# Two of four pairs of gather buffers lent to the reading of weights until four blocks are multiplied

## The chip, the core and the metric

The kernel runs on one core of one Trainium2 chip. The metric is the device time of one launch in microseconds (us); less is better. The core has TensorE (PE in the rows; PEld is its weight load), VectorE (DVE), ScalarE (ACT), GpSimd (POOL) and SyncE (SP). SP issues the large reads of weights, GpSimd issues the gathers, and all of them are carried by the same 16 DMA engines.

## What is computed

Two transformer layers on 256 tokens of width 1024, in float32. Each layer has an attention and short-convolution part (the "mixer") and then a mixture of very many tiny experts, which is where the change lies:

```python
def peer(h, w_query, sub_keys, expert_u, expert_v):
    ...
    q = (hf @ w_query).reshape(T, PEER_HEADS, 2, PEER_HALF)
    scores = jnp.einsum("thpd,hpnd->thpn", q, sub_keys).astype(jnp.float32)
    top_v, top_i = lax.top_k(scores, PEER_TOPK)
    ...
    best_v, best_pos = lax.top_k(cand_v, PEER_TOPK)
    expert_idx = jnp.take_along_axis(cand_i, best_pos, axis=-1)
    gates = jax.nn.softmax(best_v, axis=-1).astype(h.dtype)
    ...
        u = jnp.take(expert_u, xc["idx"], axis=0)
        vv = jnp.take(expert_v, xc["idx"], axis=0)
        a = jax.nn.gelu(jnp.einsum("td,thkd->thk", xc["h"], u))
        return jnp.einsum("thk,thkd->td", xc["g"] * a, vv)
```

There are 16384 experts. Each is a row of 1024 numbers in `expert_u` (the first matrix) and one in `expert_v` (the second). Each token picks 128 of them: 8 heads with 16 each.

## The kernel before, in words

The two halves of the 256 tokens are handled in two ways. Tokens 0 to 127 are multiplied densely: all of the first matrix streams through TensorE (128 blocks of 128 experts), Gelu is taken of every product, the products are weighed by the gates, and then all of the second matrix streams through TensorE. Tokens 128 to 255 gather: for each of the 128 picks, GpSimd issues an indirect DMA that fetches one row of 4 KB for each of the 128 tokens (0.5 MB), and VectorE multiplies it; first 128 gathers of U rows in four quarters, then those of V rows, interleaved as in `GROUPS` (line 29).

**The stream of weights.** `stream` (lines 108 to 146) is the list of all weight loads in the order of their use. Its unit is a group of 1 MB (two blocks): for the expert part 8 groups of `w_query`, then 64 groups U0 to U63, then 64 groups V0 to V63. `load_ahead` (line 175) issues on SP's queue as many groups as there are buffers, and it is called again each time a group has been used up (`dense_done`, line 354). A group goes into a spare part if one fits, and otherwise into a ring of three `raw` buffers.

**Spare parts.** At the start of the expert part, memory that is needed only later is handed to the stream by `give_back` with a limit (lines 1205 to 1212). `spare_part` (line 157) lets a group take the first part, in the order of limits, whose limit is at least the group's place. The places are -8 to -1 for the 8 groups of `w_query` and 0 to 63 for U0 to U63 (line 151); V groups have none.

```python
def spare_part(i):
    if i in place:
        for j, (last, _) in enumerate(spare):
            if place[i] <= last:
                spare_of[i] = spare.pop(j)
                return spare_of[i][1]
```

The parts are eight 1 MB pieces of the two halves of the products (tiles `al` and `ah` in the rows), with limits 1, 9, 17, 25, 33, 41, 49 and 57; the four pairs of gather buffers (tile `rows`) with limit -5; and `hot` with limit 29. Parts of the same limit stand in the order in which they were handed over, the pieces of the halves first. A part that is given back can be taken again by a group whose place is within its limit.

**Gathers.** `experts` (line 954) holds the gather buffers in the list `free` (line 981), 8 of them, two in each pair. `issue` (line 983) takes as many buffers as are free and issues a gather into each, if the quarter's routing is done. `use` (line 1000) multiplies the oldest gather on VectorE (line 1005 for U, 1013 for V), frees its buffer and calls `issue`. From query block 9 on there is one `use` per block, and one per block of U.

**The order around the change.** `query` (line 911) multiplies 16 query blocks. After each, `step` (line 1047) lets VectorE do some routing (`route`, line 826: the top 16 lists, the gates, the indices), issues gathers and, from block 9 on, uses one. Then come the blocks of U (loop at line 1091): 8 matmuls each (line 1097), a share of routing while it lasts, one use; after four blocks ScalarE takes the Gelu (line 1111). When the routing is done, `factors` (line 895) turns the gates of the first half on TensorE (line 899) into `iT`, `jT` and `gT` (lines 901 and 903). From there on the products are weighed between the blocks (`weigh`, line 1073). The V loop (line 1132) follows; its loads are kept in step with the gathers by a small copy that VectorE releases (line 195).

Each engine runs its instructions in the order in which the program issues them.

Of the kernel before, what the change touches and what calls it, by code (L numbers as in the profile page):

```python
# [27 lines left out]
NROWS, MORE = 8, (1, 3)  # L28
# [18 lines left out]
def body(ctx: ExitStack, tc: tile.TileContext, d: dict, out: bass.AP):  # L47
# [11 lines left out]
    def open_h():  # L59
        split["h"] = split["stack"].enter_context(tc.tile_pool(name="hid", bufs=1))  # L60
# [6 lines left out]
    def mm_ps(shape):  # L67
        return psum.tile(shape, F32, name="mm", bufs=2)
# [86 lines left out]
    spare_of = {}  # L155
# [10 lines left out]
    def give_back(part):  # L166
        spare.append(part)
        spare.sort(key=lambda p: p[0])
# [6 lines left out]
    def load_ahead():  # L175

        while state["dma"] < len(stream):
            kind, parts = stream[state["dma"]]
            if state["dma"] < len(START):
                if state["out0"] == NRAW0:  # L180
                    return
                t = first.tile([128, 2, D], F32, name="raw0", bufs=NRAW0)
                state["out0"] += 1
            elif (t := spare_part(state["dma"])) is not None:
                pass
            elif state["out"] < NRAW:
                t = strm.tile([128, 2, D], F32, name="raw", bufs=NRAW)
                state["out"] += 1
            else:
                return  # L190
            if kind == "V" and in_step["on"]:

                mark = in_step["marks"][0:1, in_step["n"]:in_step["n"] + 1]
                in_step["n"] += 1
                V.memset(mark, 0.0)
                nc.sync.dma_start(mark, d["c"][:, 0:1])
            for s, ap in parts:
                nc.sync.dma_start(t[:, s], ap)
            raws[state["dma"]] = t
            state["dma"] += 1  # L200
# [52 lines left out]
    def tick():  # L253
        due = [x for x in later if x[0] <= 0]
        for x in due:
            later.remove(x)
            x[1]()
        for x in later:
            x[0] -= 1
# [6 lines left out]
    def gate_begin(l, r):  # L266
        acc = work.tile([128, D], F32, name=f"acc{r}")
        G.memset(acc, 0.0)
        nc.gpsimd.dma_start(acc[0:1], d["b_gate"][l, r:r + 1])
        acc_of[l, r] = acc  # L270
# [75 lines left out]
    def dense(kind):  # L346

        while isinstance(stream[state["unit"] // 2][0], tuple):
            next_unit()
        g = state["unit"] // 2  # L350
        assert stream[g][0] == kind and state["unit"] % 2 == 0
        return raws[g]

    def dense_done():
        g = state["unit"] // 2
        raws.pop(g)
        state["unit"] += 2
        if g in spare_of:
            give_back(spare_of.pop(g))
        else:  # L360
            state["out"] -= 1
        load_ahead()
# [5 lines left out]
    def fill(budget):  # L368
        credit[0] = min(credit[0] + budget, 4000.0)
        while bg and credit[0] > 0:  # L370
            cost = next(bg[0], -1)
            if cost is None:
                return
            if cost < 0:
                bg.popleft()
            else:
                credit[0] -= cost
# [253 lines left out]
    def norm_full(l, xps, hf):  # L631

        rr = rms_row()
        keep_warm(WARM[2])
        raw = dense("query")
        pss = [y_ps([128, S]) for _ in range(2)]
        for k in range(KD):
            z = work.tile([128, S], F32, name="hf", bufs=4)
            V.scalar_tensor_tensor(z, xps[k // 2][:, k % 2], acol[:, l, 1, k:k + 1], rr, op0=OP.mult, op1=OP.mult)
            A.activation(hf[:, k], z, AF.Identity, bias=adac[:, l, 2, k:k + 1])  # L640
            for x in range(2):
                T.matmul(pss[x], raw[:, x, k * 128:(k + 1) * 128], hf[:, k], start=(k == 0), stop=(k == KD - 1))
        dense_done()
        return pss
# [309 lines left out]
    def experts(es, xp, rp, low, halves, pairs, hot, l, hf, pss):  # L954
# [23 lines left out]
        ys = []  # L978
        seen = {"dve": False}

        free = deque(pair[:, i] for i in range(2) for pair in pairs)

        def issue():
            while tasks and free and tasks[0][1] in routed:
                assert not any(last < 0 for last, _ in spare_of.values())
                kind, q, s = tasks.popleft()
                t = free.popleft()
                s += 32 * q
                G.indirect_dma_start(out=t, out_offset=None, in_=rows[kind],  # L989
                                     in_offset=bass.IndirectOffsetOnAxis(ap=idx[:, s:s + 1], axis=0))  # L990
                flying.append((kind, q, s, t))
# [8 lines left out]
        def use():  # L1000
            if not flying:
                return
            kind, q, s, t = flying.popleft()
            if kind == "U":
                V.scalar_tensor_tensor(t, t, 1.0, h1, op0=OP.mult, op1=OP.mult, accum_out=av[:, s:s + 1])  # L1005
                if s % 32 == 31:
                    c = slice(32 * q, 32 * q + 32)
                    after(6, lambda: A.activation(cv[:, c], av[:, c], AF.Gelu_apprx_tanh))
                    after(9, lambda: weights(q))
            else:  # L1010
                assert q in ready_c
                if seen["dve"]:
                    V.scalar_tensor_tensor(y1, t, cv[:, s:s + 1], y1, op0=OP.mult, op1=OP.add)  # L1013
                else:
                    V.tensor_scalar(y1, t, cv[:, s:s + 1], None, op0=OP.mult)
                    seen["dve"] = True
            free.append(t)
            issue()
# [72 lines left out]
        for e in range(0, NE, 4):  # L1091
            ps = mm_ps([128, 4, 128])
            for u in range(0, 4, 2):
                raw = dense("U")
                for x in range(2):
                    for k in range(KD):
                        T.matmul(ps[:, u + x], raw[:, x, k * 128:(k + 1) * 128], hf[:, k, :128],  # L1097
                                 start=(k == 0), stop=(k == KD - 1))
                    if bg:
                        fill(1350)  # L1100
                    elif e >= 64:
                        i = e + u + x
                        while done[0] < 34 and done[0] * (NE - begun[0]) < 35 * (i + 1 - begun[0]):
                            next(weighing, None)
                            done[0] += 1
                    if bg or e < 64:
                        begun[0] = e + u + x + 1
                    use()
                    tick()
                dense_done()  # L1110
            A.activation(halves[e // 64][:, e % 64:e % 64 + 4], ps, AF.Gelu_apprx_tanh)  # L1111
        spare.clear()
        for _ in weighing:
# [18 lines left out]
        for e in range(0, NE, 2):  # L1132
# [19 lines left out]
            for x in range(2):  # L1152
                i = e + x
# [33 lines left out]
    for l in range(DEPTH):  # L1187
        if l:
            open_h()
        h = norm(l, 0, "qk", xps) if l else first_norm(xps)  # L1190
        gate_begin(l, 0)
        gate_begin(l, 1)
        early.close()
        pol["pool"] = POOL_MIX[l]
        with ExitStack() as es:
            xps = mixer(es.enter_context(tc.tile_pool(name="mix", bufs=1)), l, *h)
        es = ExitStack()
        xp = es.enter_context(tc.tile_pool(name="exp", bufs=1, side="right"))
        hf = xp.tile([128, KD, S], F32, name="hfull")
        split["stack"].close()  # L1200
        rp = es.enter_context(tc.tile_pool(name="route", bufs=1, side="right"))
        low = ExitStack()
        halves = [stack.enter_context(tc.tile_pool(name=f"act{n}", bufs=1, side="right", reuse_waits="tile"))
                  .tile([128, 64, 128], F32, name=f"a{n}") for n, stack in (("h", es), ("l", low))][::-1]
        for b in range(8):
            part = halves[b // 4][:, b % 4 * 16:b % 4 * 16 + 16].rearrange("p j t -> p (j t)")
            give_back((8 * b + 1, part.rearrange("p (u c) -> p u c", u=2)))
        pairs = [xp.tile([128, 2, D], F32, name=f"rows{i}") for i in range(NROWS // 2)]
        for t in pairs:
            give_back((-5, t))  # L1210
        hot = xp.tile([128, 9, 256], F32, name="hot")
        give_back((29, hot[:, :8].rearrange("p a b -> p (a b)").rearrange("p (u c) -> p u c", u=2)))
        load_ahead()
        pss = norm_full(l, xps, hf)
        xps = experts(es, xp, rp, low, halves, pairs, hot, l, hf, pss)
# [67 lines left out]
```

## Time and profile before

| | us |
|---|---|
| median of 3 runs | 1865.59 |
| lowest and highest | 1862.36, 1866.03 |
| the profiled execution's own time | 1870.19 |
| its span, first to last instruction | 1868.4 |

The mean granted clock of TensorE over the span is 0.948 of full speed. Busy shares of the span: TensorE 87%, VectorE 76%, GpSimd 51%, ScalarE 31%; the DMA engines move 669 MB, at a mean of 358 GB/s.

How to read it: an average over the whole span mixes stages that are limited by different engines. Busy times are therefore read by stretch, and a wait is read together with what ended it. Times within the execution count from the first instruction. The expert part of layer 0 lies from about 255 to 938 us; that of layer 1 starts some 907 us later.

### The profile page before, as it was taken

What the parts mean: (1) busy time and instruction counts of PE and PEld (TensorE: products, weight loads), DVE (VectorE), ACT (ScalarE), POOL (GpSimd) and SP (SyncE); (2) the same over time, 40 slices, a digit from 0 to 9 for tenths busy, and PEclk for the clock granted to TensorE, in tenths of its full rate; (3) what the DMA queues carried; (4) which work ended last, traced back from release to release, by engine and by line L of the source; (5) the groups of instructions that cost most, each with busy time, mean ns of one, the idle gap of its engine ahead of it and who ended that gap; (6) DMA issues with size and microseconds to landing.
All of it is one profiled execution on the core that took longest, in us unless ns stands there. A gap on an engine that the chain in (4) does not pass through costs nothing.

```text
span 1868.4 us, 26270 instructions
## 1 busy us (share of the span) xinstructions
PE 1620.5 (87%) x9527; PEld 1270.3 (68%) x9527; DVE 1414.8 (76%) x2723; ACT 575.8 (31%) x1257; POOL 951.1 (51%) x731
## 2 busy tenths in 40 slices
PE   6899889976879989987789999998786998988776
PEld 4779769976879744533357997898786994444322
DVE  7887859999978776655566967699997887666455
ACT  3464332211156433300046444221112654331001
POOL 3535203444579776755341231244446987776551
PEclk7899999988989999999999999999897999999999
DMA  8658788999999999999945676899999999999997
GB/s 318 252 193 320 260 336 307 404 408 409 408 391 392 409 415 416 415 415 414 410 169 198 251 288 256 327 384 408 409 404 382 389 402 415 411 416 414 415 416 283
DMA packets 163203, 669.24 MB, mean 358 GB/s; under 512 B 16001, under 2 KB 16001, under 8 KB 146690
## 3 DMA queue, kind: packets, MB, share of 16 engines
q1 hardware_dynamic: 87346, 396.39, 54.3%
q0 software_dynamic: 73856, 268.48, 36.3%
q10 hardware_dynamic: 1872, 2.69, 0.4%
q8 instruction: 75, 1.23, 0.3%
q14 instruction: 54, 0.44, 0.1%
HBM read 666.46 MB, written 1.05 MB: 357 GB/s over the span
## 4 chain that ended last, share of the span: by engine, by line
DVE 33%; DMA 29%; PE 23%; issue 6%; POOL 4%; ACT 3%; SPq 0%; POOLq 0%; ACTq 0%; DVEq 0%
DMA rows<-in_expert_v_dram,idx 16%; PE mm L1097 8%; DVE rows L1005 7%; DMA raw<-in_expert_v_dram 6%; PE yp L1155 4%; DVE raw L288 4%; DMA rows<-in_expert_rows_dram,idx 4%; PE wp L1084 3%; DVE y L1013 3%; POOL rows L989 3%; DVE wl L343 2%; PE mm L392 1%; PE mm L393 1%; PE mm L394 1%; PE mm L938 1%
## 5 line engine op out<-in xcount | busy, mean ns | idle before, releaser
L989 POOL DMA_INDIRECT rows<-in_expert_rows_dram,idx x256 | 306.8, 1198 | 335.3 <-DVE rows L1005 92.2
L989 POOL DMA_INDIRECT rows<-in_expert_v_dram,idx x256 | 329.4, 1287 | 231.5 <-DMA rows<-in_expert_v_dram,idx 95.7
L1013 DVE SCALAR_TENSOR_TENSOR y<-rows,cv,y 128x1024 f32<-128x1024 f32 x254 | 335.6, 1321 | 147.2 <-DMA rows<-in_expert_v_dram,idx 140.0
L1005 DVE SCALAR_TENSOR_TENSOR rows<-rows,h 128x1024 f32<-128x1024 f32 x256 | 329.2, 1303 | 3.5 <-DMA rows<-in_expert_rows_dram,idx 3.3
L1155 PE MATMUL yp<-raw,ah 128*128 128x512 f32 x512 | 242.3, 621 | 56.0 <-DMA raw<-in_expert_v_dram 54.8
L343 POOL TENSOR_TENSOR wl<-raw,wh 128x1024 fp32r<-128x1024 f32 x52 | 137.1, 2641 | 272.5 <-ACT wh L338 255.7
L1155 PE MATMUL yp<-raw,al 128*128 128x512 f32 x512 | 244.4, 622 | 32.1 <-DMA raw<-in_expert_v_dram 31.8
L1097 PE MATMUL mm<-hfull,raw 128*128 128x128 f32 x1984 | 241.1, 281 | 19.1 <-ACT al L1111 15.4
L1097 PEld LDWEIGHTS mm<-hfull,raw 128*128 128x128 f32 x1984 | 232.5, 196 | 19.9 <-ACT al L1111 15.8
L1069 ACT ACTIVATE hot<-iotf,iT 128x128 f32<-128x128 f32 x512 | 163.2, 390 | 262.6 <-PE wp L1084 229.0
L1155 PEld LDWEIGHTS yp<-raw,ah 128*128 128x128 f32 x512 | 96.1, 196 | 200.6 <-issue 101.3
L1097 PE MATMUL mm<-hfull,ah 128*128 128x128 f32 x1600 | 193.6, 283 | 14.9 <-ACT al L1111 14.9
L1097 PEld LDWEIGHTS mm<-hfull,ah 128*128 128x128 f32 x1600 | 190.1, 200 | 15.3 <-ACT al L1111 15.3
L1155 PEld LDWEIGHTS yp<-raw,al 128*128 128x128 f32 x512 | 95.0, 195 | 137.2 <-issue 96.9
L392 PE MATMUL mm<-hh,wh 128*128 128x256 f32 x512 | 150.4, 294 | 10.1 <-ACT qT L656 6.3
L1067 POOL TENSOR_TENSOR hot<-hot,gT 128x256 f32<-128x256 f32 x128 | 152.2, 1190 | 2.4
L1084 PEld LDWEIGHTS wp<-hot 128*128 128x128 f32 x1024 | 129.9, 193 | 32.4 <-issue 28.7
L338 ACT ACTIVATE wh<-raw 128x1024 fp32r<-128x1024 f32 x112 | 115.9, 1051 | 101.7 <-DMA raw<-in_w_gt_dram 39.4
L393 PE MATMUL mm<-hl,wh 128*128 128x256 f32 x512 | 147.1, 287 | 0.0
L394 PE MATMUL mm<-hh,wl 128*128 128x256 f32 x512 | 146.9, 287 | 0.0
L1084 PE MATMUL wp<-hot 128*128 128x64 f32 x1024 | 129.1, 270 | 2.9 <-POOL hot L1067 2.9
L343 DVE TENSOR_TENSOR wl<-raw,wh 128x1024 fp32r<-128x1024 f32 x60 | 90.8, 1521 | 36.2 <-ACT wh L338 35.4
(230 smaller groups left out, 2371.6 us busy)
## 6 DMA issues: line engine op xcount, KB each, us to landing
raw<-in_expert_v_dram SPq DMA_DIRECT2D x128, 1024.0 KB
raw<-in_expert_u_dram SPq DMA_DIRECT2D x62, 1024.0 KB
ah<-in_expert_u_dram SPq DMA_DIRECT2D x50, 1024.0 KB
raw<-in_w_adat_dram SPq DMA_DIRECT2D x64, 512.0 KB
raw<-in_w_gt_dram SPq DMA_DIRECT2D x16, 1024.0 KB
raw<-in_w_adag_dram SPq DMA_DIRECT2D x16, 1024.0 KB
raw<-in_w_cv_dram SPq DMA_DIRECT2D x12, 1024.0 KB
raw<-in_w_qk_dram SPq DMA_DIRECT2D x8, 1024.0 KB
```

Of the source, the lines that this page charges most:

```text
L343: l_engine().tensor_tensor(lo, raw, f(h), op=OP.subtract)
L392: T.matmul(ps, h[:, c], mh[:, k], start=first, stop=False)
L393: T.matmul(ps, h[:, c], ml[:, k], start=False, stop=False)
L394: T.matmul(ps, lo[:, c], mh[:, k], start=False, stop=last)
L989: G.indirect_dma_start(out=t, out_offset=None, in_=rows[kind], in_offset=bass.IndirectOffsetOnAxis(ap=idx[:, s:s + 1], axis=0))
L1005: V.scalar_tensor_tensor(t, t, 1.0, h1, op0=OP.mult, op1=OP.mult, accum_out=av[:, s:s + 1])
L1013: V.scalar_tensor_tensor(y1, t, cv[:, s:s + 1], y1, op0=OP.mult, op1=OP.add)
L1067: G.tensor_tensor(q, q, gT[:, ts, None].to_broadcast([128, TB, 64]), op=OP.mult)
L1069: A.activation(p[:, i], iotf, AF.Abs, bias=iT[:, b * TB + i:b * TB + i + 1])
L1084: T.matmul(ps[:, t], p[:, t], q[:, t], start=True, stop=True)
L1097: T.matmul(ps[:, u + x], raw[:, x, k * 128:(k + 1) * 128], hf[:, k, :128], start=(k == 0), stop=(k == KD - 1))
L1155: T.matmul(ys[q], halves[i // 64][:, i % 64], raw[:, x, q * 512:(q + 1) * 512], start=(i == 0), stop=(i == NE - 1))
```

## The change

Half of the pairs get the limit 1 in place of -5, and the gathers start with the other half alone, so with 4 buffers in place of 8. After the first four blocks of U (`e == 0`) the other four buffers join the list `free`. The assertion now says that no buffer of the first two pairs is still held by the stream when a gather is issued.

```diff
-        free = deque(pair[:, i] for i in range(2) for pair in pairs)
+        free = deque(pair[:, i] for i in range(2) for pair in pairs[:NROWS // 4])
 
         def issue():
             while tasks and free and tasks[0][1] in routed:
-                assert not any(last < 0 for last, _ in spare_of.values())
+                assert not any(any(t is p for p in pairs[:NROWS // 4]) for _, t in spare_of.values())
                 kind, q, s = tasks.popleft()
                 t = free.popleft()
...
                 dense_done()
+            if e == 0:
+                free.extend(pair[:, i] for i in range(2) for pair in pairs[NROWS // 4:])
             A.activation(halves[e // 64][:, e % 64:e % 64 + 4], ps, AF.Gelu_apprx_tanh)
...
         pairs = [xp.tile([128, 2, D], F32, name=f"rows{i}") for i in range(NROWS // 2)]
-        for t in pairs:
-            give_back((-5, t))
+        for i, t in enumerate(pairs):
+            give_back((-5 if i < NROWS // 4 else 1, t))
```

## Rows read from the trace of the kernel before

**Rows 1.** The page: the chain that ended last, by engine.

```profile
DVE 33%; DMA 29%; PE 23%; issue 6%; POOL 4%; ACT 3%; SPq 0%; POOLq 0%; ACTq 0%; DVEq 0%
```

**Rows 2.** Stretches: from:to, length, each engine's busy us, clock, DMA, GB/s.

```profile
340.00:360.00 20.00, 20.00 (x182) 20.00 (x181) 19.27 (x59) 3.17 (x5) 9.70 (x9) 1.00 1.03 409
500.00:520.00 20.00, 7.62 (x69) 7.39 (x67) 15.62 (x17) 0.60 (x1) 12.65 (x11) 0.78 1.03 409
523.00:629.00 106.00, 105.27 (x923) 105.28 (x924) 88.26 (x142) 65.82 (x171) 91.19 (x75) 0.97 1.01 392
629.00:938.00 309.00, 264.14 (x774) 128.63 (x773) 189.60 (x290) 64.13 (x166) 188.12 (x148) 0.97 1.01 412
1434.00:1540.00 106.00, 106.00 (x927) 106.00 (x926) 89.44 (x139) 65.38 (x170) 92.45 (x75) 0.97 0.99 385
```

**Rows 3.** Waits in 345:480 (two rows), 480:700 and 1400:1540: total, times, longest.

```profile
ACT sel L862 <- DVE sel L861: 59.0, 4, 17.9
...
PE mm L1097 <- ACT al L1111: 23.8, 3, 9.5
...
PE wp L899 <- DVE iT L903: 16.1, 1, 16.1
...
PE wp L899 <- DVE iT L903: 14.8, 1, 14.8
```

**Rows 4.** Tile rows: gathers of 290:437.5, then the 15th and the 19th alone.

```profile
L989 POOL DMA_INDIRECT rows<-in_expert_rows_dram,idx x61: 932/938/1682, 294.2 to 436.8; - x61
...
DMA to landing us min/median/max: 4.4/12.7/17.3
...
L989 POOL DMA_INDIRECT rows<-in_expert_rows_dram,idx x1: 1679/1679/1679, 323.7 to 323.7; - x1
...
DMA to landing us min/median/max: 6.1/6.1/6.1
...
L989 POOL DMA_INDIRECT rows<-in_expert_rows_dram,idx x1: 936/936/936, 333.1 to 333.1; - x1
...
DMA to landing us min/median/max: 9.8/9.8/9.8
```

**Rows 5.** The chain in order of time, layer 0 and layer 1: start, us, what.

```profile
436.84 17.07 DMA rows<-in_expert_rows_dram,idx
...
453.94 1.23 DVE rows L1005 x2
...
1344.71 18.73 DMA rows<-in_expert_rows_dram,idx
```

**Rows 6.** SP's queue in order of time, layer 0: start, first to last issue, count.

```profile
253.28 0.37 SPq L198 DMA_DIRECT2D rows<-in_w_query_dram  x1
253.70 2.26 SPq L198 DMA_DIRECT2D al<-in_w_query_dram  x4
...
256.55 9.48 SPq L198 DMA_DIRECT2D ah<-in_expert_u_dram  x4
266.13 16.41 SPq L198 DMA_DIRECT2D raw<-in_expert_u_dram  x3
305.58 15.97 SPq L198 DMA_DIRECT2D al<-in_expert_u_dram  x3
326.00 0.37 SPq L198 DMA_DIRECT2D hot<-in_expert_u_dram  x1
```

**Rows 7.** Stretches around the first gathers of layer 0, columns as in rows 2.

```profile
290.00:295.00 5.00, 5.00 (x29) 4.48 (x28) 4.66 (x17) 1.42 (x4) 0.76 (x1) 1.00 0.01 3
290.00:342.70 52.70, 52.61 (x352) 49.12 (x351) 50.40 (x159) 13.64 (x28) 24.61 (x23) 1.00 0.85 323
```

**Rows 8.** VectorE in order of time: the first, twelfth and sixteenth use of a gather.

```profile
299.98 1.21 DVE L1005 SCALAR_TENSOR_TENSOR rows<-rows,h 128x1024 f32<-128x1024 f32 x1
...
335.13 1.21 DVE L1005 SCALAR_TENSOR_TENSOR rows<-rows,h 128x1024 f32<-128x1024 f32 x1
...
343.76 1.21 DVE L1005 SCALAR_TENSOR_TENSOR rows<-rows,h 128x1024 f32<-128x1024 f32 x1
```

## The prediction, made before the changed kernel ran

> **What bounds the kernel now.** I read the page for the span and the chain that ended last, the table of stretches to see which engine is full where, the waits to see what stops whom, and then one layer's load queue, gathers and VectorE in order of time.
>
> The chain gives VectorE, DMA and TensorE a third to a quarter each [rows 1], so it must be read by stretch. In the expert part of layer 0 [rows 2] there are three stretches. Up to 523 us DMA runs at 409 GB/s and VectorE is busy 19.3 of 20 us, with routing and one gather use per block; at its end TensorE works only 7.6 of 20 us. From 523 to 629 TensorE is full (105.3 of 106 us) and DMA has a little room (392). From 629 to 938 DMA is full at 412. The work goes from one to the next: TensorE stands still for 16.1 us until VectorE has made iT (L903), and 14.8 us in the other layer [rows 3]. Before that it stood still on ScalarE (23.8 us), whose queue waited for VectorE's sel (59.0 us). So the end of the first stretch is VectorE's; what delays VectorE there delays the layer, while the stream of U blocks may be late by some 16 us.
>
> VectorE's own waits look small, but it runs on the edge of the gathers. Of the first 61 gathers of layer 0 [rows 4] the 19th, issued at 333.1, took 9.8 us to land, at 342.9. The 61st, issued at 436.8, took 17.07 us: it landed at 453.9, and its use began at 453.94 [rows 5]. Between the two landings lie 42 gathers in 111.0 us, 2.64 us each: 0.524 MB in 2.64 us is 199 GB/s, about half of the 409, the other half being the stream's. The gathers' lead over VectorE has been eaten up by then; in layer 1 the chain shows the same, 18.73 us from 1344.71 on.
>
> **The change, part by part.** *Who gets which buffer.* By the code a buffer takes the next group whose place is at most the buffer's limit; queries have places -8 to -1, U groups from 0. Today [rows 6] the raw ring holds queries 1 to 3, one pair query 4, the quarters of al queries 5 to 8, hot U0, ah U1 to U4; U5 to U7 go to the raw ring from 266 us on. U8 to U10 go to quarters of al as queries 6 to 8 are done (three issues from 305.58 on), U11 to hot at 326.00. With limit 1 on two pairs, query 5 still takes al's first quarter, queries 6 and 7 take these pairs, query 8 the quarter with limit 9; so U0 and U1 go to al's last quarters, U2 to hot, U3 to U6 to ah, U7 to U9 to the raw ring. Two groups more are read ahead. But the buffers of queries 5 to 8 then have limits of 1 and 9 and cannot take U10, so nothing is issued between U9 (282) and 326: by 326 the change has issued one group fewer.
>
> *Stream.* In 290 to 295 the DMA moves 3 GB/s [rows 7]. The two more groups (2.1 MB, 5.1 us at 409 GB/s) fill this hole. This is worth nothing at the end by itself, as TensorE is not short of stream there (the 16 us above).
>
> *First gather.* It lands 4.4 us after its issue at 294.24 today, and its use begins at 299.98 [rows 4, 8]: 1.3 us to spare. With a stream packet beside it the 15th gather took 6.1 us [rows 4]. That would be 0.4 us late at worst; I take 0, as the hole is longer than the two groups.
>
> *Four gather buffers less until the first four U blocks are done.* Gathers 1 to 4 go out as now. Each use then issues one, so gather 5 is issued after use 1 (now gather 9 is), and so on to gather 15 after use 11. The twelfth use begins at 335.13 [rows 8] and is the first after the four buffers come back, so it issues gathers 16 to 20; with some 1.2 us of use and 0.3 us of issue that is 336.6. With the 6.1 us of the 15th gather, gather 16 lands at 342.7, just before its use at 343.76 [rows 8]. Up to there VectorE loses nothing, as the gathers run ahead of the stream's next load. But at 342.9 the 19th landed today: the queue is now three gathers behind, and from there on it is served 2.64 us apiece. That is 7.9 us by the count. At the 61st gather, which has no lead, VectorE is late by it.
>
> The count is too much where the stream's buffers are full during a TensorE stop and the gathers get the whole rate. The bytes bound this: 323 GB/s over 52.7 us [rows 7] are 17.0 MB today. With the change: 2.1 MB of stream in the hole, 16 gathers of 0.524 (8.4 MB), 0.3 of keys, and stream again from 328 on: 14.7 us at 409 is 6.0 MB, less some 4.5 gathers (2.4), 3.6 MB. That is 14.4, a lack of 2.6 MB, or 6.3 us at 409 GB/s. Since DMA is full until 523, I take 6.3 us per layer, the bytes' value, nearest to what a full DMA must make up; 7.9 stays as one bound, and 0 (later reads make it up) as the other.
>
> *A page's rule against the row.* The row: a gather took 6.1 us beside little traffic and 17.07 us in the full stretch [rows 4, 5]. The Trainium skill (DMA: Bandwidth & Descriptors, section Anatomy of one DMA) gives a DMA of this path 2.0 us plus its bytes at 436 GB/s. For 0.524 MB that is an estimate of 3.2 us. By it four gathers in flight would be as good as eight and the sum would be 0; the trace disagrees where DMA is full.
>
> *Edits at nothing.* The assertion and the list slice run while the program is built. The instruction order of each engine is the same but for the places of POOL's gather issues and of the loads on SP's queue; SP passes the new loads in the place of old ones after 253.28, when the mixer has ended. If it had to wait there for a buffer, queries 6 and 7 would still have some 50 us. A wait of POOL before gather 16 has only gathers behind it. TensorE then begins its full stretch (106 us in either layer, rows 2) and the 412 GB/s stretch later by the same time; neither has room to make it up.
>
> Sum: 2 x 6.3 = 12.6 us later. The profiled execution took 1870.19 us (span 1868.4), 4.6 us above the median of 1865.59; against the median I forecast 1865.6 + 12.6 = 1878.2 us. A measurement of this kernel tells about 0.2% (3.7 us) from no change.
>
> **Rivals.**
> 1. *Hidden.* The gathers land in time with four buffers, or make up the lack when the stream is full. For it: VectorE loses nothing before 343, and the stream is ahead at each TensorE stop. Against: the lead at the 61st gather is nil in both layers. Time: 1865.6 us, to 1869. The page's formula would lead here too.
> 2. *Faster: the reads ahead count.* Place: the hole at 290 us in each layer. If the U stream set the first stretch's end, 2.1 MB earlier would save 5.1 us per layer: 1855.4 us. It decides if TensorE waits for a U load, not for iT, at 507 to 523; the 16.1 us wait for iT speaks against it, and so does the group lost at 326.
> 3. *Worse: all four gathers stay missing.* If the queue never makes up any and the fourth is lost too, 4 x 2.64 = 10.6 us per layer: 1886.7 us. For it: two queues at half rate each leave no room. Against: gather 16 takes the place of the 19th, not of the 20th.
> 4. *The change does not do what it says.* The freed pairs hold query blocks and not U blocks, by the walk through the limits. This is part of the forecast; were they to hold U0 and U1, with the quarters of al taken up again, the lack would be one group smaller: 1.05 MB, 2.6 us per layer, so 1873.0 us.
>
> **How the numbers follow.** Forecast (5 to 7.9 us per layer) 0.50; rival 4 or a partly made up lack 0.16; rival 3 0.14; rival 1 0.13; rival 2 0.07. Slower by over 0.2%: 0.50 + 0.16 + 0.14 and a little of rival 1, 0.82; within 0.2% 0.11; faster 0.07. The range leaves out rival 2 and half of rival 1, and reaches past rival 3: 1867 to 1888 us. The forecast's own range is 1875 to 1882.
>
> **What the profile after would show.** SP's queue: two query loads into rows, the issues of 266 to 282 followed by none until 326. The hole at 290 to 295 filled, a new one of low DMA between 296 and 326. POOL: four gathers at 294, then single ones, then five together near 336.6. VectorE: waits for expert_rows gathers of some 5 to 8 us in all between 343 and 460, where there are next to none; TensorE's wait for iT ends near 530 in place of 523.7, and the start of the V stretch moves with it, by the same in layer 1. The prediction is wrong if VectorE's waits for gathers stay under 2 us per layer, or if the wait for iT ends no later, or if TensorE waits for U loads.

## The result, and the profile after

| | us |
|---|---|
| before, median of 4 runs | 1864.37 (1862.36 to 1866.03) |
| after, median of 4 runs | 1881.85 (1876.84 to 1883.52) |
| ratio, 95% interval | 1.0084 (1.0066 to 1.0102) |
| the profiled execution after, and its span | 1883.52, 1881.8 |

The change makes the kernel slower. By the ratio it is 15.7 us (12.3 to 19.0), where 12.6 us were forecast; the spans of the two profiled executions differ by 13.4 us. The page after: span, busy time of each engine, and the chain that ended last by engine.

```profile
span 1881.8 us, 26275 instructions
...
PE 1611.0 (86%) x9527; PEld 1260.0 (67%) x9527; DVE 1409.7 (75%) x2723; ACT 575.3 (31%) x1257; POOL 934.3 (50%) x731
...
DMA 33%; DVE 24%; PE 22%; issue 8%; POOL 7%; ACT 3%; SPq 0%; POOLq 0%; DVEq 0%; ACTq 0%
```

No engine has more to do. In the chain VectorE's share has gone from 33% [rows 1] to 24% and DMA's from 29% to 33%: work that VectorE used to do without a stop now waits for something that DMA brings. The averages say no more, so the stretches come next.

**Where the time lies.** I cut each layer's expert part at three matmuls: the first of the first stretch (L642), the last that waits for iT (L899), and the first of the V stretch. TensorE in order of time after, layer 0 and then layer 1; what ended an idle time stands in brackets.

```profile
258.57 3.72 PE L642 MATMUL yp<-hfull,raw 128*128 128x256 f32 x16 [0.36 <-ACT hfull L640]
...
533.21 0.48 PE L899 MATMUL wp<-ident,sel 128*128 128x128 f32 x1 [15.62 <-DVE iT L903]
...
1446.13 0.48 PE L899 MATMUL wp<-ident,sel 128*128 128x128 f32 x1 [14.98 <-DVE iT L903]
```

The same two rows of layer 0 before:

```profile
257.22 5.01 PE L642 MATMUL yp<-hfull,raw 128*128 128x256 f32 x22 [0.37 <-ACT hfull L640]
...
523.73 0.48 PE L899 MATMUL wp<-ident,sel 128*128 128x128 f32 x1 [16.10 <-DVE iT L903]
```

So the first stretch takes 533.21 - 258.57 = 274.6 us in place of 266.5, 8.1 more. In layer 1, cut in the same way, it takes 274.2 in place of 268.5, 5.7 more. The rest is as before: from L899 to the V stretch 107.0 and 109.1 us (107.7 and 108.5), the V stretch 314.1 and 315.9 (315.6 and 315.8), the mixer of layer 1 217.7 (218.0), the tail 10.6 (10.6). The two first stretches hold 13.8 us, about as much as the spans differ by (13.4). TensorE still waits about as long for iT as before [rows 3]: what it waits for there is VectorE, not a read of the stream.

**What became of the reads.** SP's queue after, layer 0: start, time over which the issues spread, destination and source, count.

```profile
254.63 0.37 SPq L198 DMA_DIRECT2D rows<-in_w_query_dram  x1
255.05 0.46 SPq L198 DMA_DIRECT2D al<-in_w_query_dram  x1
255.56 1.13 SPq L198 DMA_DIRECT2D rows<-in_w_query_dram  x2
256.73 0.47 SPq L198 DMA_DIRECT2D al<-in_w_query_dram  x1
257.25 1.68 SPq L198 DMA_DIRECT2D al<-in_expert_u_dram  x2
...
273.82 10.07 SPq L198 DMA_DIRECT2D raw<-in_expert_u_dram  x3
327.35 3.94 SPq L198 DMA_DIRECT2D al<-in_expert_u_dram  x2
```

Two of the three loads into `rows` are the lent pairs, and they hold query blocks; no U block ever lies in them. Two groups of U start at once in their stead, the ring is full at 283.9, and then nothing is issued for 43 us. Stretches, columns as in [rows 2]; the first row is of before, the others of after:

```profile
296.00:326.00 30.00, 29.91 (x171) 27.04 (x170) 28.56 (x97) 8.23 (x19) 15.05 (x15) 1.00 0.94 350
...
290.00:295.00 5.00, 5.00 (x27) 4.46 (x26) 4.66 (x14) 0.38 (x1) 0.00 (x0) 1.00 1.03 407
296.00:326.00 30.00, 29.91 (x165) 26.88 (x164) 28.59 (x98) 8.58 (x21) 10.50 (x11) 1.00 0.58 186
...
533.00:639.00 106.00, 105.79 (x935) 105.80 (x936) 89.16 (x142) 65.73 (x171) 93.26 (x75) 0.99 1.01 399
640.00:946.00 306.00, 262.87 (x755) 126.00 (x755) 186.87 (x289) 64.18 (x167) 187.45 (x148) 0.97 1.02 413
```

The hole of before at 290 to 295, 3 GB/s [rows 7], is filled (407), and 296 to 326 has become the hole: 186 GB/s, where the trace of before shows 350. GpSimd issues 11 instructions there instead of 15. The later stretches run much as they did [rows 2] and take as long, so no time is made up in them.

**What became of the gathers.** GpSimd in order of time after; the idle time before each, and what ended it, in brackets. These are the 5th and then the 15th to the 20th gather.

```profile
302.81 1.25 POOL L989 DMA_INDIRECT rows<-in_expert_rows_dram,idx  x1 [2.45 <-DVE rows L1005]
...
334.45 0.94 POOL L989 DMA_INDIRECT rows<-in_expert_rows_dram,idx  x1 [2.58 <-DVE rows L1005]
335.69 0.94 POOL L989 DMA_INDIRECT rows<-in_expert_rows_dram,idx  x1 [0.30 <-issue]
336.94 1.56 POOL L989 DMA_INDIRECT rows<-in_expert_rows_dram,idx  x1 [0.30 <-issue]
338.81 0.95 POOL L989 DMA_INDIRECT rows<-in_expert_rows_dram,idx  x1 [0.30 <-issue]
340.06 0.94 POOL L989 DMA_INDIRECT rows<-in_expert_rows_dram,idx  x1 [0.30 <-issue]
341.31 0.94 POOL L989 DMA_INDIRECT rows<-in_expert_rows_dram,idx  x1 [0.30 <-issue]
```

From the 5th on GpSimd waits for VectorE to hand back a buffer; when the other four come, five gathers go out in a row. In the trace of before, the 19th was issued at 333.1 and the 61st at 436.8 [rows 4]; after, the 19th goes out at 340.06, and the 61st at 445.1. VectorE pays: its first wait for a gather of U rows, and the sum of these waits in the first stretch of layer 0 and of layer 1 (total, times, longest).

```profile
340.13 1.22 DVE L1005 SCALAR_TENSOR_TENSOR rows<-rows,h 128x1024 f32<-128x1024 f32 x1 [0.78 <-DMA rows<-in_expert_rows_dram,idx]
...
DVE rows L1005 <- DMA rows<-in_expert_rows_dram,idx: 6.4, 12, 0.9
...
DVE rows L1005 <- DMA rows<-in_expert_rows_dram,idx: 4.7, 10, 0.8
```

Before, VectorE had no such wait in layer 0 and 1.5 us of them in layer 1. From 331 on the chain of waits goes through the gathers. One link of it after, start, us, what:

```profile
426.29 19.05 DMA rows<-in_expert_rows_dram,idx
...
445.36 1.23 DVE rows L1005 x2
```

The gather took 19.05 us and was used as soon as it was there. The Trainium skill (DMA: Bandwidth & Descriptors, section Anatomy of one DMA) would have had these 0.524 MB there in an estimated 3.2 us, by which four buffers would have done as well as eight; here too the measurement decides against it.

### The profile page after: what moved, and what is told of

Its sections match the earlier page's. It is cut to its first block, busy times and chain, and to the rows that moved or that the text cites. A ratio compares the mean times of both kernels' runs of the same rounds, so it can differ in the third digit from the quotient of the medians.

```text
span 1881.8 us, 26275 instructions
## 1 busy us (share of the span) xinstructions
PE 1611.0 (86%) x9527; PEld 1260.0 (67%) x9527; DVE 1409.7 (75%) x2723; ACT 575.3 (31%) x1257; POOL 934.3 (50%) x731
## 4 chain that ended last, share of the span: by engine, by line
DMA 33%; DVE 24%; PE 22%; issue 8%; POOL 7%; ACT 3%; SPq 0%; POOLq 0%; DVEq 0%; ACTq 0%
DMA rows<-in_expert_v_dram,idx 15%; DMA rows<-in_expert_rows_dram,idx 10%; PE mm L1097 8%; POOL rows L989 5%; DMA raw<-in_expert_v_dram 4%; DVE rows L1005 4%; PE wp L1084 3%; DVE y L1013 3%; PE yp L1157 3%; DVE raw L288 2%; DVE wl L343 2%; POOL hot L1067 1%; PE mm L392 1%; DMA raw<-in_w_gt_dram 1%; PE mm L938 1%
## 5 line engine op out<-in xcount | busy, mean ns | idle before, releaser
L989 POOL DMA_INDIRECT rows<-in_expert_rows_dram,idx x256 | 296.1, 1157 | 358.6 <-DVE rows L1005 105.4
L1097 PE MATMUL mm<-hfull,raw 128*128 128x128 f32 x1920 | 233.7, 281 | 23.9 <-ACT al L1113 21.1
L1097 PEld LDWEIGHTS mm<-hfull,raw 128*128 128x128 f32 x1920 | 226.0, 197 | 24.7 <-ACT al L1113 21.5
L1097 PE MATMUL mm<-hfull,ah 128*128 128x128 f32 x1600 | 192.2, 280 | 20.1 <-ACT al L1113 15.8
L338 ACT ACTIVATE wh<-raw 128x1024 fp32r<-128x1024 f32 x112 | 115.9, 1051 | 109.1 <-DMA raw<-in_w_gt_dram 43.1
```

## The experiments

Two questions were open: whether the loss comes from the buffers that the gathers lack or from the stream that is one group behind, and whether its size follows the bytes, as I had taken, or the count of gathers that the queue is behind. Each kernel was timed against the kernel before; the edits of e1 to e4, e6, e11 and e12 are shown against the changed kernel, those of e5 and e7 to e10 against the kernel before. "Stretches" is what both first stretches take more than in the trace of before (535.0 us together, one execution each); "total" is the ratio times the median of before, less that median.

The last column takes up the bytes. It was read from the same traces after all runs, and forecast none of them. The prediction's sum ended at 342.7 us, which is 85.5 us after the first matmul of the stretch (257.22). Up to that point TensorE has done nearly the same work in all kernels but e5 (491 to 512 matmuls), so what the DMA has carried less by then is hardly a result of the delay. "DMA short" is that lack in both layers together, as the time it takes at 409 GB/s; 1 GB/s in one layer is 0.2 us. The 85.5 us of layer 0 in before, after, e1, e2, e4 and e9:

```profile
257.22:342.72 85.50, 84.40 (x512) 77.31 (x513) 65.84 (x221) 21.91 (x50) 24.62 (x23) 1.00 0.91 351
...
258.57:344.07 85.50, 84.33 (x508) 76.89 (x508) 65.10 (x218) 21.93 (x50) 22.27 (x22) 1.00 0.84 316
...
260.28:345.78 85.50, 84.39 (x512) 77.43 (x513) 64.44 (x218) 21.91 (x50) 22.53 (x21) 1.00 0.86 325
...
258.17:343.67 85.50, 84.40 (x512) 77.31 (x513) 65.89 (x220) 21.93 (x50) 24.50 (x23) 1.00 0.90 339
...
258.50:344.00 85.50, 84.39 (x512) 77.43 (x513) 65.87 (x220) 21.91 (x50) 22.54 (x21) 1.00 0.88 328
...
259.10:344.60 85.50, 84.39 (x512) 77.41 (x513) 65.87 (x220) 21.92 (x50) 24.59 (x23) 1.00 0.92 351
```

| kernel | stretches, us | ratio (95% interval) | total, us | DMA short, us |
|---|---|---|---|---|
| after | +13.8 | 1.0084 (1.0066, 1.0102) | +15.7 | 14.4 |
| e1: four buffers, stream as before | +11.9 | 1.0063 (1.0045, 1.0081) | +11.8 | 10.7 |
| e2: buffers back at block 13 | +5.4 | 1.0028 (1.0016, 1.0040) | +5.2 | 5.0 |
| e3: one pair lent | +4.4 | 1.0031 (1.0016, 1.0047) | +5.8 | 5.6 |
| e4: pairs hold U | +9.5 | 1.0081 (1.0063, 1.0099) | +15.1 | 10.5 |
| e5: pairs in turn, first attempt | +27.5 | 1.0169 (1.0148, 1.0190) | +31.5 | 24.9 |
| e6: change, two parts less | +14.3 | 1.0118 (1.0101, 1.0135) | +22.0 | 21.1 |
| e7: before, two parts less | +3.2 | 1.0052 (1.0036, 1.0069) | +9.7 | 11.7 |
| e8: before, one part less | +0.3 | 1.0016 (0.9997, 1.0036) | +3.0 | 5.9 |
| e9: hole filled, nothing lost | -1.4 | 1.0008 (0.9995, 1.0022) | +1.5 | 0.0 |
| e10: pairs in turn | +0.9 | 1.0022 (1.0012, 1.0033) | +4.1 | 3.1 |
| e11: four buffers, back at block 13 | +1.9 | 1.0029 (1.0013, 1.0045) | +5.4 | 3.1 |
| e12: four buffers, back after eight blocks | +9.1 | 1.0066 (1.0050, 1.0081) | +12.3 | 10.2 |

In e9 to e12, timed together, the total is each time some 3 us above the stretches (2.9 to 3.5). The profiled execution of before was itself 4.6 us above its median, so the column of stretches can carry an offset of that size. That of e2 was the slowest of its ten (5.4 us above their median), that of e4 the fastest of its four (4.1 below): differences of a few us between stretches are not safe.

The DMA's lack lies within the interval of the total in all kernels but e4 (10.5 us; the interval begins at 11.8) and e5, where TensorE itself stood still. The count, 2.64 us for each place in the gather queue and layer (three places in after, e1, e4, e6 and e12, one in e3, none in the others), lies outside it in e1, e2, e6, e7, e10, e11 and e12, in e1 and e12 only just (15.8 us; both intervals end at 15.1).

**e1: the buffers alone.** All four pairs keep their limit, so the stream is that of before; the gathers start with four buffers as in the change.

```diff
-            give_back((-5 if i < NROWS // 4 else 1, t))
+            give_back((-5, t))
```

> Gathers start with four buffers and get the other four after the first four U blocks, but all four pairs keep the limit -5, so the stream of weights is as before. Theory (the four missing buffers put the gather queue some three gathers behind at the point where DMA becomes full, and VectorE pays for it): slower than before by about the changed kernel's own loss, 8 to 16 us; sixteenth gather issued near 336, VectorE waits for gathers by the 61st. Rival (the loss comes from the stream: pairs with limit 1 make al's quarters unusable, and one group is issued less by 326): no loss here, within 3 us of before.

The stretches take 11.9 us more, the total is 11.8. VectorE's waits for U gathers in layer 0 and layer 1, and TensorE's wait for iT in layer 0:

```profile
DVE rows L1005 <- DMA rows<-in_expert_rows_dram,idx: 6.7, 10, 1.8
...
DVE rows L1005 <- DMA rows<-in_expert_rows_dram,idx: 7.9, 10, 1.4
...
PE wp L899 <- DVE iT L903: 13.2, 1, 13.2
```

The missing buffers alone bring most of the loss, and the same wait. The change adds 1.9 us of stretches to it, 3.9 in the totals, whose intervals overlap, and 3.7 by the bytes: that is what is left for the stream.

**e2: the change with the buffers back early.** The reads are those of the change, but the other four buffers join the list at query block 13, with the stream's hole still ahead.

```diff
         def step(n):
             fill(3600 if n < 9 else 2400)
+            if n == 13:
+                free.extend(pair[:, i] for i in range(2) for pair in pairs[NROWS // 4:])
             issue()
...
-            if e == 0:
-                free.extend(pair[:, i] for i in range(2) for pair in pairs[NROWS // 4:])
```

> As the changed kernel, limits too, but the four buffers come back after query block 13 (in layer 0 near 313 us) instead of after the first four U blocks (near 333). Theory: the gathers catch up while DMA has room (186 GB/s between 296 and 326 in the changed kernel), so the loss goes: within 4 us of before, and faster by some us if the two groups read ahead count for anything. Rival (the stream): the loss stays, 13 to 17 us.

5.2 us in total (3.0 to 7.5) and 5.4 in the stretches: about a third of the change's loss stays when the buffers come back before the DMA is full again. The gathers are then level: in layer 0 the 40th lands 141.8 us after the first matmul (141.6 before), and VectorE's 50th use is 0.1 us later in either layer. What is missing is one group of the stream (12 GB/s in 85.5 us, 1.0 MB per layer), and the loss is about its bytes. It shows later: VectorE's 64th use is 2.0 and 0.5 us behind in the two layers, the end of the stretch 4.0 and 1.4. That the loss is the stream's is not shown by this total alone, as e11 (below) loses as much without that group.

**e3: one pair lent instead of two.** The gathers start with six buffers.

```diff
-        free = deque(pair[:, i] for i in range(2) for pair in pairs[:NROWS // 4])
+        free = deque(pair[:, i] for i in range(2) for pair in pairs[:3])
...
-                free.extend(pair[:, i] for i in range(2) for pair in pairs[NROWS // 4:])
+                free.extend(pair[:, i] for i in range(2) for pair in pairs[3:])
...
-            give_back((-5 if i < NROWS // 4 else 1, t))
+            give_back((-5 if i < 3 else 1, t))
```

> One pair lent instead of two: six gather buffers until the first four U blocks are done. Theory: the eighteenth gather takes the place that the sixteenth has in the changed kernel, so the queue is one gather behind and not three: 2.6 us per layer, 3 to 6 us slower than before in all. Rival (the stream): by the walk through the limits no issue is lost here by 326, so no loss, or half of the changed kernel's, 7 to 8 us, if the loss goes with the number of pairs.

4.4 us of stretches, 5.8 in total, and VectorE's waits for U gathers are 3.9 and 3.4 us in the two layers, between those of before and of after. The loss is larger with four buffers lent than with two.

**e4: the pairs really hold U blocks.** Queries are kept out of the lent pairs, and these get limits that let them hold U0 and U1. The quarters of `al` are then taken up again.

```diff
-                if place[i] <= last:
+                if place[i] <= last and not (place[i] < 0 and last % 1):
...
-            give_back((-5 if i < NROWS // 4 else 1, t))
+            give_back((-5 if i < NROWS // 4 else i - 1.5, t))
```

> As the changed kernel, but the two lent pairs may take only U0 and U1, not query blocks. Queries 5 to 8 go to al's quarters as before, and two quarters can be taken up again before 326 (U10 and U11), so the stream has one group more than before by 326 where the changed kernel has one less. Gathers as in the changed kernel. Theory by bytes (what counts is the sum that DMA lacks): 1.6 MB of gathers less 1.0 MB of stream, 0.5 MB or 1.3 us per layer, 3 us slower than before. Theory by count (only the gather queue's own place counts): 12 to 16 us slower, as the changed kernel. Rival (the stream alone): no loss or a gain.

SP's queue and the same 30 us of e4:

```profile
257.31 1.62 SPq L198 DMA_DIRECT2D rows<-in_expert_u_dram  x2
...
314.66 8.17 SPq L198 DMA_DIRECT2D al<-in_expert_u_dram  x2
...
296.00:326.00 30.00, 29.91 (x166) 26.93 (x165) 28.59 (x97) 8.50 (x20) 10.46 (x11) 1.00 0.70 235
```

By 326 this stream has issued twelve U groups, two more than the change, but as many as before, whose twelfth goes out at 326.00 [rows 6]. The walk in the expectation stopped one step too early: before issues its 13th group 72.4 us after the first matmul and its 14th 75.9 us after it, e4 its 13th only at 75.9. From there on e4 is a group behind before, and GpSimd issues 11 instructions in these 30 us, as in the change. Its DMA is short by 10.5 us, not by the 3 of the theory by bytes, so this run does not decide between bytes and count. Against the change it saves 4.3 us of stretches, about what its bytes say (14.4 - 10.5), but only 0.6 in the totals.

**e5 and e10: all pairs lent one after another.** Each pair gets a limit of its own, so that its query block is multiplied early and its two buffers come back before the gathers need them.

```diff
-        free = deque(pair[:, i] for i in range(2) for pair in pairs)
+        free = deque(pair[:, i] for pair in pairs for i in range(2))
...
-        for t in pairs:
-            give_back((-5, t))
+        for i, t in enumerate(pairs):
+            give_back((i - 5, t))
```

> All four pairs are lent and come back one after another: limits -5, -4, -3 and -2, so they hold queries 4 to 7, and all eight gather buffers are in the list from the start, pair by pair; a gather waits only until its pair's query blocks are multiplied (by 290, 298, 306 and 313 us in layer 0). Three groups more are read ahead than before by 290, none lost by 326, one issue 3.6 us late after that. Theory (gathers missing when DMA becomes full cost the time, reading ahead is worth little): gathers land as before by 342, so within 3 us of before. Rival (early reads of the stream harm in themselves, as the loss of 5 us that stayed with the early return could be read): 5 to 8 us slower.

This first attempt (e5) tells nothing on the question. The program issues the gathers into the later pairs ahead of the query matmuls that read those pairs, so these multiply gathered rows in place of some blocks of `w_query`: it computes something else, and TensorE waits for the gathers. Its wait in the query part of layer 0:

```profile
PE mm L938 <- DMA rows<-in_expert_rows_dram,idx: 12.3, 1, 12.3
```

In e10 the list starts empty, and each pair joins it once its query block is multiplied:

```diff
-        free = deque(pair[:, i] for i in range(2) for pair in pairs)
+        free = deque()
...
+            if n in (7, 9, 11, 13):
+                free.extend(pairs[(n - 7) // 2][:, i] for i in range(2))
...
-        for t in pairs:
-            give_back((-5, t))
+        for i, t in enumerate(pairs):
+            give_back((i - 5, t))
```

> All four pairs hold queries 4 to 7 (limits -5 to -2), and each joins the gather buffers only after the step in which its query blocks have been multiplied (n = 7, 9, 11 and 13). Three groups more are read by 290 than before, one fewer is issued after 326. Theory: gathers land as before by 342 and the stream is level by then, so within 4 us of before. Rival (four gathers fewer at 294 to 313 cost as in the changed kernel): 8 us or more slower.

Stretches +0.9 us, total +4.1 (2.2 to 6.1). The hole is filled (407 GB/s from 288 to 293), but another one opens between 296 and 326 (256 GB/s, 350 before). All eight buffers are there by block 13, VectorE's 40th use is 0.1 us later than before in either layer, the DMA is 3.1 us short, and nothing is won.

**e6, e7, e8: less read ahead.** A theory that came up after e4: if reads ahead bring nothing, fewer of them should leave the gathers more of the DMA. e6 takes the last two parts of `ah` from the change, e7 takes them from the kernel before, and e8 takes one.

```diff
-            give_back((8 * b + 1, part.rearrange("p (u c) -> p u c", u=2)))
+            if b < 6:
+                give_back((8 * b + 1, part.rearrange("p (u c) -> p u c", u=2)))
```

(For e8 the condition is `b < 7`.)

> The changed kernel with two of the four 1 MB pieces of ah not handed to the stream, so its reads run two groups less ahead through most of the U blocks. Theory (a gather is served at half the rate as long as the stream has anything to load, so what hurts is the stream's backlog beside the gathers): the gather queue gets the full rate sooner, the loss shrinks to 4 to 11 us over before. Rival (bytes: DMA lacks 2.1 MB more per layer): the loss grows by 5 us per layer, to 24 to 27 us over before.

> The kernel of before with two of the four pieces of ah not handed to the stream. Theory: VectorE's waits for gathers (5.3 and 7.1 us between the first query block and iT in the two layers) shrink, so 3 to 10 us faster than before, as long as TensorE does not wait for U loads. Rival (bytes): 5 us per layer slower, 10 us in all.

> As the run before, with one piece of ah left out. Theory: half of that gain, 1 to 5 us faster. Rival (bytes): 2.6 us per layer slower, 5 us in all.

The theory falls: none is faster than the kernel that it starts from. e6 is some 6 us slower than the change (22.0 and 15.7, the intervals just overlap), e7 9.7 us slower than before, and e8 3.0, which its interval does not tell from nothing. Two groups are 2.1 MB per layer, 10.3 us for both layers at 409 GB/s, so e7 loses about their bytes. Its gathers are not late: VectorE waits for rows of U 1.1 us in layer 0 and not at all in layer 1. TensorE's waits in e7, layer 0:

```profile
PE wp L899 <- DVE iT L903: 10.1, 1, 10.1
...
PE mm L1097 <- DMA raw<-in_expert_u_dram: 6.8, 8, 1.2
```

A part of the wait for iT has become a wait for U loads. Most of e7's loss (9.7 - 3.2 us) lies outside the first stretches, part of it behind them: from L899 to the V stretch 109.9 and 109.5 us in place of 107.7 and 108.5, the V stretch 316.6 and 318.0 in place of 315.6 and 315.8. The stream's lead is thus not free to take, and bytes that the stream lacks cost time as well as those that the gathers lack.

**e9: the hole filled and nothing lost.** One pair takes the fifth query block and comes back at block 9, before the gathers can use it, so that one more group of U starts at the outset; the six other buffers are there from the start.

```diff
-        free = deque(pair[:, i] for i in range(2) for pair in pairs)
+        free = deque(pairs[j][:, i] for i in range(2) for j in (0, 2, 3))
...
         def step(n):
             fill(3600 if n < 9 else 2400)
...
+            if n == 9:
+                free.extend(pairs[1][:, i] for i in range(2))
...
-        for t in pairs:
-            give_back((-5, t))
+        for i, t in enumerate(pairs):
+            give_back((-4 if i == 1 else -5, t))
```

> One pair lent, with limit -4, so that it holds query 5 and frees a quarter of al for U0; it comes back after query block 9 (near 298 us), before any gather needs it. One group is read in the hole at 290 us, and U9 to U11 are issued at 313, 321 and 326 as before: nothing is lost by 326 and no gather is later. Theory (what the early return kept of the loss was the one group issued less by 326, and a group read earlier is worth nothing by itself): within 3 us of before. Rival (filling the hole harms the first gathers): 3 to 6 us slower. Rival (the hole is worth its bytes): 2.6 us per layer, 5 us faster.

1.0008 (0.9995 to 1.0022), and the stretches 1.4 us shorter. The stretch of low DMA in e9 and the wait for iT:

```profile
290.00:295.00 5.00, 5.00 (x27) 4.47 (x26) 4.69 (x14) 0.38 (x1) 0.00 (x0) 1.00 0.71 279
...
PE wp L899 <- DVE iT L903: 16.2, 1, 16.2
```

Most of the hole is filled with a read of the first matrix (what is left lies at 292 to 297, 121 GB/s), TensorE waits for iT as before, and the time is that of before. But the lead does not last: from 315 to 320 the DMA of e9 moves 261 GB/s (410 before), and after 85.5 us it has carried what it carries before (351 GB/s in both). So a filled hole is worth nothing by itself; what a lead that lasts would be worth, this run cannot say. No version was faster than before; this one is the nearest to an equal.

**e11 and e12: the moment of return.** Both are e1 (the stream of before) with another time at which the four buffers come back: at query block 13 (e11, the edit of e2), or after eight U blocks instead of four (e12).

```diff
-            if e == 0:
+            if e == 4:
```

> As the run with four gather buffers and all limits -5, but the other four come back after query block 13 (near 313 us). Theory: the gathers catch up before DMA is full, nothing else is changed, so within 3 us of before; the 5 us that the early return left with the changed limits then belong to the stream's lost group. Rival (a gather issued late is late for good): 10 us slower, as with the return after four U blocks.

> As the run with four gather buffers and all limits -5, but the other four come back after eight U blocks instead of four. Theory (three gathers behind when they come back after four blocks; the queue then serves one per 2.64 us, so at most the fourth is lost as well): 1 to 3 us per layer more than that run's 12 us, 14 to 18 us slower than before. Rival (the delay grows with the time of the return): four uses later at 2.9 us each, 12 us per layer more, 30 us or more slower.

e12: 9.1 us of stretches, 12.3 in total (9.3 to 15.1), no more than e1's 11.9 and 11.8. VectorE's waits for U gathers, layer 0 and layer 1:

```profile
DVE rows L1005 <- DMA rows<-in_expert_rows_dram,idx: 6.3, 10, 1.2
...
DVE rows L1005 <- DMA rows<-in_expert_rows_dram,idx: 6.6, 10, 1.1
```

So the loss does not grow with the time for which the buffers are away: the DMA is as short as in e1 (10.2 and 10.7 us), and with four buffers it loses nothing more once it is full. In e11 the stretches lose 1.9 us, and its total of 5.4 (2.4 to 8.4) is more than the theory's 3 and less than the rival's 10. VectorE's 50th use is 0.1 us later than before, and the DMA is 3.1 us short. The rest of the theory, that what stayed in e2 belongs to the stream's lost group, cannot be read from the totals, as e11 without that loss ends at 5.4 and e2 at 5.2; the bytes (3.1 and 5.0) and the stretches (1.9 and 5.4) differ, the latter by one execution each.

## Why the prediction was right, and where it was off

*What bounds the kernel* was right: the end of the first stretch is VectorE's. In after, e1, e3, e4 and e12 TensorE waits for iT for 12 to 16 us, though it ends later than before. What was drawn from it, that the stream "may be late by some 16 us", holds for the first stretch at most: in e7, where only the stream has less, the wait for iT shrinks and the two first stretches lose 3.2 us, but the kernel loses 9.7.

*Who gets which buffer* was right to the group: queries 6 and 7 in the lent pairs, U7 to U9 in the ring by 284, then nothing until 327. The change in its own words, reads of the first matrix in gather buffers, does not take place; rival 4 described this as part of the forecast. Its other half, that with U blocks in the pairs the lack would be a group smaller, shows in the bytes (14.4 and 10.5 us) but not in the time: the 7.4 us of that rival lie below e4's interval (11.8 to 18.5).

*The hole is worth nothing*, and *the first gather costs nothing*: right as far as it was tried. e9 fills the hole, and its time is that of before, but so are its bytes; in after VectorE's first wait for U rows is at the 14th gather.

*Four buffers less until four blocks are done*: mechanism and place were right, and the size within the interval. Measured were 8.1 and 5.7 us, 6.9 in the mean, between the 6.3 by bytes and the 7.9 by count. The count tells how late VectorE becomes in the first stretch: at its 64th use it is 8.6 and 7.1 us behind in after, 7.6 and 7.2 in e1, 7.3 and 6.6 in e4, 7.3 and 5.9 in e12, whatever the stream did. What the whole kernel loses goes rather with the bytes: e2, e7 and e10 have no gather missing when the DMA becomes full and lose 5.2, 9.7 and 4.1 us, near what their DMA is short by (5.0, 11.7, 3.1). So the choice of the bytes' value for the sum is borne out, though not to the last us: e4 loses more than its bytes.

The term that was mis-sized is the lack. The sum had 14.4 MB in place of 17.0, 2.6 less; the DMA carried 3.0 and 2.9 MB less in the two layers (35 and 34 GB/s in 85.5 us). With these the sum is 14.4 us and not 12.6, nearer to the measured 15.7. That 12.6 lies just inside the interval (12.3 to 19.0) has some luck in it.

*The five gathers of the return* were issued from 335.69 to 341.31, one every 1.25 to 1.9 us. I had put them at 336.6 together; I had left out GpSimd's issue time, some 5 us for the last of them. Whether that cost anything was not tried.

*The later stretches pass the delay on*: right, 107 to 109 and 314 to 316 us, as before (108 to 109 and 316).

*Rivals.* Hidden: fallen, VectorE waits, and the interval excludes no change. Faster by reads ahead: fallen here, as TensorE waits for iT and not for a U load; none of e4, e9 and e10 gained either, but in none of them had the DMA carried more than before by the 85.5 us. All four places stay missing (21.1 us): above the interval, and e12 shows that being away longer adds nothing.

Open are why the loss in the two layers differs (8.1 and 5.7) and why e4's total is above both its bytes and its stretches; that its profiled execution was 4.1 us below its median is a part of the latter.

## What to carry to other kernels

A buffer lent to one queue is taken from another. Where the DMA becomes full and stays nearly so, count what all queues together have carried by that moment: here this lack, at the full rate, came near the loss of nearly every version, whichever queue it was that lacked. Filling an idle stretch of the DMA is worth something only if the lead is still there at that moment. And walk the allocation by its own rules, to the end, before believing what a change says that it does: here the lent buffers never held what they were meant for, and in e4 the walk stopped one group too early.

## What was unexpected

Reads taken away cost about their bytes, and a hole filled brought nothing. Two groups less cost 9.7 us (e7; 10.3 at 409 GB/s), while one group read into the hole gave the time of before (e9: 0.9995 to 1.0022), because the same bytes were missing from the DMA 30 us later.

VectorE could use little of the room that the gathers regained. In layer 0 of e1, counted from the first matmul of the stretch, the 41st gather landed 10.2 us later than before (154.5 against 144.3 us) and the 47th 5.8 (165.8 against 160.0), so they had caught up by some 4 us in between. VectorE's lag stayed at 7.6 to 7.7 us from the 40th to the 61st use: it works through its queue in order and is busy almost all of the time (51.0 of 53 us from 412 to 465), so a gather that is early again helps it little. In layer 1, where VectorE of before waits for the 61st gather itself, the lag fell from 9.0 to 7.2 us.
